# Eleven Strassen pairs instead of eight, their weight sums formed by adding transfers, in a two-layer decoder trunk

## The chip, the cores and the metric

One core of one Trainium2 chip runs the whole program; the other cores are idle. The metric is device microseconds of one execution. The kernel before takes 1021.03 us, the median of three runs (1020.96 to 1021.89).

## The reference, cut to what matters

Two layers over 256 tokens of width 1024, all in fp32. Each layer is a half-step SwiGLU feed-forward, a token mixer beside a cross-attention to a memory, and a second half-step SwiGLU; a last RMSNorm follows. The change touches the four feed-forwards and the first and last microseconds.

```python
D_MODEL, SEQ, DEPTH, D_FF = 1024, 256, 2, 2816

def rmsnorm(x, g, eps=1e-6):
    return x * lax.rsqrt(jnp.mean(x * x, axis=-1, keepdims=True) + eps) * g

def swiglu(h, w_up, w_down):
    gate, up = jnp.split(h @ w_up, 2, axis=-1)
    return (jax.nn.silu(gate) * up) @ w_down

for i in range(DEPTH):
    x = x + 0.5 * swiglu(rmsnorm(x, norm_g[i, 0]), ffn_w_up[i, 0], ffn_w_down[i, 0])
    h = rmsnorm(x, norm_g[i, 1])
    x = x + mixer(h, mem)        # layer 0: causal pooling, layer 1: differential attention
    x = x + 0.5 * swiglu(rmsnorm(x, norm_g[i, 2]), ffn_w_up[i, 1], ffn_w_down[i, 1])
return rmsnorm(x, final_norm_g)
```

## The kernel before, in words

**Precision.** Every fp32 weight and activation is split into hi (rounded to fp32r by ScalarE) and lo (the rest, by VectorE). A product is three matmuls: hi by hi, hi by lo, lo by hi (`mm3`, L474).

**Weights.** They arrive in pieces of 1 MiB (128 partitions x 2048 floats), issued on SyncE's queue into three buffers named `raw`, and are split in two halves of 1024 columns each, a CAST on ScalarE and a subtraction on VectorE, into one of four pairs of buffers `hi` and `lo` (`WB = 4`). So a split may run ahead of its use by four pieces at most. The class `Weights` (L248) keeps the queue of pieces.

**A feed-forward** has eleven chunks of 256 hidden columns. A `single` chunk (L855) takes two pieces of up-projection and 48 matmuls of 512 columns, for both halves of the tokens. Its gate (Silu on ScalarE, a multiply on VectorE) is transposed and split, and a `down` step (L846) of one piece and 24 matmuls adds the chunk to the four accumulators.

**A pair** (L758) does two chunks by seven products instead of eight (a Strassen-Winograd scheme over 2 token halves, 2 halves of the inner dimension and 2 chunks): 7 x 12 = 84 matmuls where two singles take 96. With the four weight blocks b11, b12 (first inner half of the two chunks), b21 and b22 (second half), product 1 takes b11, 5 takes b11+b12, 6 takes b11+b12+b22, 4 takes the sum of all four, 7 takes b12+b22, 2 takes b21 and 3 takes b22. VectorE forms these sums in place, eight additions of 1024 columns for a pair (L442, L1356), in four blocks held in three borrowed activation buffers (`ROOM`, tags `qk` and `mq`) and one `raw`. The activations have five sums of their own (`column_sums`, L581), which need both halves' `rstd`, the row scale of RMSNorm, made from a sum of squares by two small instructions on GpSimd (L484). Each feed-forward has two pairs (`steps`, L886): eight in all.

**The order of the work.** PE, ScalarE, VectorE and SyncE run in the order in which Python emits instructions. A planner (`Clock`, L57, with a duration for each kind of instruction, and `Flow`, L197) decides that order from chains of steps with due times. GpSimd's order is left to a scheduler of its own. A tile's readers and writers wait for each other through semaphores.

**Begin and end.** `begin` (L917) runs eight warm-up matmuls on zeros while the first pieces land (`BEGIN`, `BEGIN_X`, L44). At the end `accumulate` (L667) makes the last 512 columns of each token half in two parts of 256, and `last` (L1325) adds, squares and scales each part.

Of the kernel before, what the change touches and what calls it, by code (L numbers as in the profile page):

```python
# [18 lines left out]
P = 128  # L19
# [19 lines left out]
HOLD_PIECE = "hold"  # L39
# [3 lines left out]
WARM = 8  # L43
BEGIN = ((0, 1), (1, 2), (2, 4), (4, 8))  # L44
BEGIN_X = {0: (1, 4), 2: (4, 8)}
MARGIN = 0.25
LEFT = 384
BACKLOG = 0.3
# [81 lines left out]
class Engine:  # L130
# [117 lines left out]
class Weights:  # L248
# [3 lines left out]

    def __init__(self, flow, load, run, free):
        self.flow, self.load, self.run, self.free = flow, load, run, free
        self.queue, self.raw, self.done = [], {}, {}
        self.loaded = self.started = self.live = 0
        self.running = False
        self.open = []

    def add(self, key, src, tag="raw", pre=None, post=None, frees=("raw",)):  # L260
        self.queue.append((key, src, tag, pre, post, frees))

    def give(self, **tags):
        self.free.update(tags)
        self.pump()

    def pump(self):
        while self.loaded < len(self.queue):
            key, src, tag = self.queue[self.loaded][:3]
            if src is not None:  # L270
                if not self.free[tag]:
                    break
                self.free[tag] -= 1
                self.raw[key] = self.load(key, src, tag)
            self.loaded += 1
        if self.running or self.started >= self.loaded:
            return
        key, _, _, pre, _, _ = self.queue[self.started]
        if pre is HOLD_PIECE:
            self.started += 1  # L280
            self.pump()
            return
        if isinstance(key, tuple):
# [4 lines left out]
        self.flow.add(self.first(self.queue[self.started]))  # L288

    def first(self, entry):  # L290

        key, _, _, pre, _, _ = entry
        if pre:
            yield from self.after(key)
        self.open.append(key)
        raw, before = pre(self.raw) if pre else (self.raw.get(key), None)
        rest = yield from self.run(key, raw, before)
        self.started += 1
        self.running = False
        self.flow.add(self.second(entry, rest))  # L300
        self.pump()

    def after(self, key):

        while self.open and self.open[0] != key:
            yield self.flow.now + 0.05

    def second(self, entry, rest):
        key, _, _, _, post, frees = entry
        self.done[key] = yield from rest  # L310
        if post:
            yield from self.after(key)
            yield from post(self.raw)
        self.open.remove(key)
        for tag in frees:
# [14 lines left out]
def trunk(ctx, tc, I, out):  # L330
# [69 lines left out]
    def raw_tile(tag="raw"):  # L400
        if tag == "raw":
            return wp.tile([P, PIECE], F32, tag="raw", name=nm("raw"), bufs=RB)
        return act.tile([P, PIECE], F32, tag=tag, name=nm("raw"), bufs=ROOM[tag])
# [14 lines left out]
    def load(key, src, tag):  # L418
        if key == "x":
            for t in range(NT):  # L420
                nc.sync.dma_start(x[:, t, :], src[:, t, :])
            return None
        raw = raw_tile(tag)
# [8 lines left out]
    def split_piece(key, raw, before):  # L432
# [23 lines left out]
    W = Weights(F, load, split_piece, {"raw": RB, "none": 1, **ROOM})  # L456
# [163 lines left out]
    def finish_part(t, s, i, ss, y, fg):  # L620

        xs = x[:, t, s]
        junk = tmp.tile([P, D], BF16, tag="junk", name=nm("junk"), bufs=1)
        nc.scalar.activation(junk[:, s], xs, AF.Square, scale=D ** -0.5, accum_out=ss[:, i:i + 1])
        nc.vector.tensor_mul(y[:, s], xs, fg[:, s])

    def finish(t, ss, y):
        v = sm.tile([P, 2], F32, tag="v2", name=nm("v"))
        r = sm.tile([P, 1], F32, tag="rstd", name=nm("rstd"))
        nc.gpsimd.tensor_scalar(v[:, 0:1], ss[:, 0:1], EPS, ss[:, 1:2], op0=ALU.add, op1=ALU.add)  # L630
        nc.gpsimd.tensor_scalar(v[:, 1:2], ss[:, 2:3], v[:, 0:1], None, op0=ALU.add)
# [35 lines left out]
    def accumulate(acc, t, lh, ll, pc, k0, first, end=None):  # L667


        fine = end is last  # L670
        for i in range(4):
            kk, h = (i % 2, i // 2) if end else (i // 2, i % 2)
            if fine and h == 1:
                break
# [3 lines left out]
            if end and kk == 1:  # L678
                end(t, acc[t], h) if not fine else end(t, acc[t], h, None)
        for part in range(2 if fine else 0):  # L680
            o = slice(part * FC, part * FC + FC)
            w = slice(512 + part * FC, 512 + part * FC + FC)
            for kk in range(2):
                mm3(acc[t][1][:, o], lh[:, k0 + kk, cols(t)], ll[:, k0 + kk, cols(t)], pc[0][:, kk, w], pc[1][:, kk, w],
                    False, kk == 1, part == 1)
                F.poll()
            end(t, acc[t], 1, part)

    def exp_table():
        nc.scalar.activation(dcol2, dcol, AF.Exp)  # L690
        yield F.now

    def ffn(layer, f, end, begin=None, exp_next=False):
# [64 lines left out]
        def pair(a, *between):  # L758
# [63 lines left out]
            downs(between[0])  # L822
# [3 lines left out]
            downs(between[1])  # L826
# [35 lines left out]

        if begin:
# [22 lines left out]
    def steps(begin):  # L886


        if begin:
            return [("single", 1), ("down", 0), ("single", 2), ("down", 1), ("single", 3), ("pair", 4, 2, 3), ("single", 6),  # L890
                    ("down", 4), ("pair", 7, 5, 6), ("single", 9), ("down", 7), ("single", 10), ("down", 8, 9, 10)]
        return [("single", 0), ("single", 1), ("down", 0), ("single", 2), ("pair", 3, 1, 2), ("single", 5),
                ("down", 3, 4), ("single", 6), ("pair", 7, 5, 6), ("single", 9), ("down", 7), ("single", 10),
                ("down", 8, 9, 10)]

    def out_proj(cat, name, chain_ids, end):
# [8 lines left out]
        W.give(**ROOM)  # L905
# [11 lines left out]
    def begin():  # L917
# [11 lines left out]
        nc.scalar.dma_start(xr2[:, 0:SEQ], I["x_cols"][:, 0:SEQ])  # L929
        nc.scalar.activation(silu, mhalf[:, 0:1], AF.Silu)  # L930
        for i, (k0, k1) in enumerate(BEGIN):
            s = slice(k0 % 4 * 512, (k1 - 1) % 4 * 512 + 512)
            nc.sync.dma_start(raw[k0 // 4][:, s], I["ffn_w_up"][0, 0, 0, k0 // 4][:, s])
            if i in BEGIN_X:
                s = slice(BEGIN_X[i][0] * SEQ, BEGIN_X[i][1] * SEQ)
                nc.sync.dma_start(xr2[:, s], I["x_cols"][:, s])
        for k in range(KT):
# [216 lines left out]
    def pool_mix(end):  # L1154
        W.free.update(qk=0, mq=0)
# [123 lines left out]
    def diff_mix(end):  # L1279
        W.free.update(qk=0, mq=0)  # L1280
# [44 lines left out]
    def last(t, acc, h, part):  # L1325

        if h == 0:
            outs[t] = (sm.tile([P, 3], F32, tag="ss3", name=nm("ss3"), bufs=2), raw_tile()[:, 0:D])
        s = half(0) if h == 0 else slice(512 + part * FC, 512 + part * FC + FC)
        a = acc[h] if h == 0 else acc[h][:, part * FC:part * FC + FC]  # L1330
        nc.vector.scalar_tensor_tensor(x[:, t, s], a, 0.5, x[:, t, s], op0=ALU.mult, op1=ALU.add)
        finish_part(t, s, h + (part or 0), *outs[t], gains[0])
        if part == 1:
            finish(t, *outs[t])

    def plan_ffn(layer, f, begin=False):
# [6 lines left out]
        def pair(a, *between):  # L1343


            key = (layer, f, "pair", a)
            b11, b12, b22, b21 = [key + (n,) for n in (1, "b12", "b22", 2)]

            def plus(of, other):
                return lambda raw: (raw[of], raw[other])  # L1350

            def all_four(raw):
                for s in range(0, PIECE, SPLIT):
                    sl = slice(s, s + SPLIT)
                    yield max(at(raw[b21][:, sl], raw[b11][:, sl]), idle("dve"))
                    nc.vector.tensor_add(raw[b21][:, sl], raw[b21][:, sl], raw[b11][:, sl])  # L1356

            W.add(b11, up[layer, f, a, 0], "qk", frees=())
            W.add(b12, up[layer, f, a + 1, 0], "qk", HOLD_PIECE)
            W.add(key + (5,), None, pre=plus(b11, b12), frees=())  # L1360
            W.add(b22, up[layer, f, a + 1, 1], "mq", HOLD_PIECE)
            downs(between[0])
            W.add(key + (6,), None, pre=plus(b11, b22), frees=())
            downs(between[1])
            W.add(b21, up[layer, f, a, 1], post=all_four, frees=("qk",))
            W.add(key + (7,), None, pre=plus(b12, b22), frees=("qk",))
            W.add(key + (3,), None, pre=lambda raw: (raw[b22], None), frees=("mq",))
            W.add(key + (4,), None, pre=lambda raw: (raw[b21], None))

        for kind, *js in steps(begin):  # L1370
# [7 lines left out]
            if begin and kind == "single" and js[0] == 1:  # L1378
                W.add("x", I["x"].rearrange("b (t p) d -> p (b t) d", p=P), "none", frees=())
# [98 lines left out]
```

## Time and profile before

| | |
|---|---|
| median of three runs | 1021.03 us |
| the profiled execution | 1020.7 us |
| its span on the core | 1019.0 us |
| granted TensorE clock, mean | 0.996 |
| DMA, mean over the span | 185 GB/s |

The profile is of one execution. A row of busy time gives the microseconds in which an engine executed something, its share of the span and its instructions. A matmul row on PE shows how long the instruction was in the pipeline (some 0.39 us for 512 columns); consecutive ones overlap, so what one costs is read from a run of them in the chain of waits. PEclk is the granted share of TensorE's clock. In a timeline, brackets hold the idle time before an instruction and what ended it.

### The profile page before, as it was taken

The page shows a single profiled execution, that of the slowest core. Times are in us where ns is not written, and L with a number is a line of the kernel's source. Part 1 is how long each engine was busy: PE and PEld are TensorE (multiplying, and loading weights), DVE is VectorE, ACT ScalarE, POOL GpSimd, SP SyncE. Part 2 cuts the span into 40 slices and gives each one's busy share as a digit, 9 for nine tenths or more (in the row PEclk, how much of TensorE's full clock was granted, in tenths as well). Part 3 has the DMA queues.
Part 4 walks back from the last instruction along what each step waited for, and adds up shares of the span by engine and source line. Part 5 has one row for each costly group of instructions (what it writes and reads, how often), then busy time and mean ns, then how long its engine had stood idle before and what let it go on. Part 6 is the DMA issues. An engine that isn't in the chain of part 4 may idle for free.

```text
span 1019.0 us, 13188 instructions
## 1 busy us (share of the span) xinstructions
PE 1004.6 (99%) x5084; PEld 850.0 (83%) x5084; DVE 766.3 (75%) x1011; ACT 599.3 (59%) x949; POOL 66.1 (6%) x125
## 2 busy tenths in 40 slices
PE   8999999999999999999999999999999999999996
PEld 7888888899888888888888888889998888888885
DVE  5989896675768886975889698555776768987963
ACT  6656565864666564656646465563676575665642
POOL 1000072200000000000000000010211000000000
PEclk9999999999999999999999999999999999999999
DMA  9745445655437255374824627444424445273341
GB/s 355 279 164 230 172 165 209 233 184 191 168 138 289 83 218 214 111 261 146 330 83 161 252 100 272 165 169 175 152 98 156 170 169 237 83 307 146 131 179 42
DMA packets 27407, 188.19 MB, mean 185 GB/s; under 512 B 3152, under 2 KB 3664, under 8 KB 5200
## 3 DMA queue, kind: packets, MB, share of 16 engines
q1 hardware_dynamic: 26768, 186.79, 49.3%
q8 instruction: 40, 0.66, 0.3%
q10 hardware_dynamic: 576, 0.56, 0.2%
q14 instruction: 23, 0.19, 0.1%
HBM read 186.29 MB, written 1.05 MB: 184 GB/s over the span
## 4 chain that ended last, share of the span: by engine, by line
PE 94%; DVE 2%; ACT 1%; POOL 1%; issue 1%; DMA 1%; POOLq 0%; ACTq 0%
PE mm L146 51%; PE acc L146 32%; PE tr L146 11%; DVE lo L146 1%; ACT ds L146 1%; DMA x_cols<-in_x_cols 1%; DVE ds L146 0%; ACT junk L146 0%; POOL rs L146 0%; DVE x_res L146 0%; POOL nmx L146 0%; DVE dw L146 0%; DVE on L146 0%; DVE cat_lo L146 0%; DVE raw L146 0%
## 5 line engine op out<-in xcount | busy, mean ns | idle before, releaser
L146 DVE TENSOR_TENSOR lo<-raw,hi 128x1024 fp32r<-128x1024 f32 (+1 forms) x398 | 470.9, 1211 | 104.8 <-ACT hi L146 104.0
L146 ACT CAST hi<-raw 128x1024 fp32r<-128x1024 f32 (+1 forms) x398 | 400.1, 1039 | 206.5 <-DVE raw L146 73.2
L146 PE MATMUL mm<-hi,xT 128*128 128x512 f32 x1120 | 357.5, 392 | 0.0
L146 PEld LDWEIGHTS mm<-hi,xT 128*128 128x128 f32 x1120 | 210.3, 188 | 43.0
L146 PE MATMUL mm<-lo,xT 128*128 128x512 f32 x560 | 218.0, 389 | 0.0
L146 PE MATMUL acc<-hi,gh 128*128 128x512 f32 (+1 forms) x356 | 140.1, 393 | 2.3 <-DVE x_res L146 2.3
L146 PE MATMUL acc<-hi,gl 128*128 128x512 f32 (+1 forms) x356 | 138.0, 388 | 0.0
L146 PE MATMUL acc<-lo,gh 128*128 128x512 f32 (+1 forms) x356 | 137.8, 387 | 0.0
L146 PEld LDWEIGHTS mm<-lo,xT 128*128 128x128 f32 x560 | 105.2, 188 | 21.0
L146 PEld LDWEIGHTS acc<-hi,gh 128*128 128x128 f32 x356 | 66.9, 188 | 15.5 <-DVE x_res L146 2.7
L146 PEld LDWEIGHTS acc<-hi,gl 128*128 128x128 f32 x356 | 66.8, 188 | 13.8
L146 PEld LDWEIGHTS acc<-lo,gh 128*128 128x128 f32 x356 | 67.0, 188 | 13.0
L146 DVE TENSOR_TENSOR raw<-raw,raw 128x1024 f32<-128x1024 f32 x64 | 76.4, 1226 | 0.0
L146 PE MATMUL mm<-xT,hi 128*128 128x256 f32 x384 | 72.0, 288 | 1.1 <-DVE mq L146 1.1
L146 PEld LDWEIGHTS mm<-xT,hi 128*128 128x128 f32 x384 | 59.6, 191 | 2.9 <-issue 1.3
L146 POOL TENSOR_SCALAR v<-ss 128x1 f32<-128x1 f32 (+1 forms) x24 | 8.9, 370 | 740.9 <-ACT junk L146 740.7
L146 ACT ACTIVATE g<-mm,rstd 128x256 f32<-128x256 f32 x62 | 29.3, 473 | 44.2 <-PE mm L146 44.1
L146 PE MATMUL mm<-xT,lo 128*128 128x256 f32 x192 | 54.3, 283 | 0.0
L146 ACT CAST gh<-tr 128x256 fp32r<-128x256 f32 (+1 forms) x60 | 26.8, 480 | 46.6 <-PE tr L146 46.6
L146 DVE SCALAR_TENSOR_TENSOR g<-mm,rstd,g 128x256 f32<-128x256 f32 x62 | 29.8, 480 | 31.6 <-ACT g L146 31.6
L146 DVE TENSOR_TENSOR gl<-tr,gh 128x256 fp32r<-128x256 f32 (+1 forms) x60 | 31.2, 542 | 14.8 <-ACT gh L146 14.7
L146 PE MATMUL acc<-hi,cat_hi 128*128 128x512 f32 x96 | 38.4, 400 | 0.0
(183 smaller groups left out, 1234.4 us busy)
## 6 DMA issues: line engine op xcount, KB each, us to landing
raw<-in_ffn_w_up SPq DMA_DIRECT2D x87, 1024.0 KB, 4.9
raw<-in_ffn_w_down SPq DMA_DIRECT2D x44, 1024.0 KB, 4.9
raw<-in_diff_w_in SPq DMA_DIRECT2D x14, 1024.0 KB, 4.8
raw<-in_mem_w_kv SPq DMA_DIRECT2D x8, 1024.0 KB, 4.8
raw<-in_pool_w_in SPq DMA_DIRECT2D x6, 1024.0 KB, 4.8
raw<-in_pool_w_out SPq DMA_DIRECT2D x6, 1024.0 KB, 4.8
raw<-in_diff_w_out SPq DMA_DIRECT2D x6, 1024.0 KB, 4.8
x_res<-in_x SPq DMA_DIRECT2D x2, 512.0 KB, 7.8
```

Of the source, the lines that this page charges most:

```text
L146: return call(*args, **kwargs)
```

## The change

It does five things. (1) `steps` has three pairs instead of two in each feed-forward but the first, so eleven in all; two down steps stand between products of every pair, as before. (2) The sums of weights are made by transfers: SyncE loads one block, and a transfer issued by GpSimd adds another block to it in SBUF (`accum_op=ALU.add`). Block sum 5 grows into 6 and then into 4, each addition being issued when the sum before it has been split; sum 7 has a buffer of its own. The blocks b11, b21 and b22 are loaded by themselves as well. VectorE's additions are gone. (3) `begin` loads the first columns of x ahead of the first weights, in finer pieces, all on SyncE, and nine warm-up matmuls run. (4) The last 512 columns are done whole. (5) The planner has a duration for the adding transfer.

```diff
+WARM = 9
+BEGIN = (("x", 0, 1), ("w", 0, 1), ("w", 1, 2), ("x", 1, 2), ("w", 2, 4), ("x", 2, 4), ("w", 4, 6), ("x", 4, 8),
+         ("w", 6, 8))
+SUMS_FROM = 35.0
...
+        if op == "dma_start" and "accum_op" in kwargs:
+            t = c.run("pool", 1.2, outs, ins) + 9.0
+            c.mark(t, t, outs, ins)
+            return
...
-            if before is not None:
-                yield max(at(raw[:, sl], before[:, sl]), idle("dve"))
-                nc.vector.tensor_add(raw[:, sl], raw[:, sl], before[:, sl])
...
+    def weight_sums(layer, f, a, before):
+        up = I["ffn_w_up"][layer, f]
+        key = (layer, f, "pair", a)
+        def begun(tag, n, first, second):
+            t = act.tile([P, PIECE], F32, tag=tag, name=nm("sum_w"), bufs=ROOM[tag])
+            nc.sync.dma_start(t, up[first])
+            nc.gpsimd.dma_start(t, up[second], accum_op=ALU.add)
+            W.raw[key + (n,)] = t
+            return t
+        def ended(*keys):
+            while not all(k in W.ended for k in keys):
+                yield F.now + 0.2
+        if len(before) > 1:
+            yield from ended(before[-2] + (4,))
+        x1 = begun("qk", 5, (a, 0), (a + 1, 0))
+        if before:
+            yield from ended(before[-1] + (7,))
+        begun("mq", 7, (a + 1, 0), (a + 1, 1))
+        for n, then, other in ((5, 6, (a + 1, 1)), (6, 4, (a, 1))):
+            yield from ended(key + (n,))
+            nc.gpsimd.dma_start(x1, up[other], accum_op=ALU.add)
+            W.raw[key + (then,)] = x1
...
+        pairs = [step[1] for step in steps(begin) if step[0] == "pair"]
+        for i, a in enumerate(pairs):
+            F.add(weight_sums(layer, f, a, [(layer, f, "pair", p) for p in pairs[:i]]), SUMS_FROM if begin else 0)
...
-        return [("single", 0), ("single", 1), ("down", 0), ("single", 2), ("pair", 3, 1, 2), ("single", 5),
-                ("down", 3, 4), ("single", 6), ("pair", 7, 5, 6), ("single", 9), ("down", 7), ("single", 10),
-                ("down", 8, 9, 10)]
+        return [("single", 0), ("single", 1), ("pair", 2, 0, 1), ("single", 4), ("down", 2), ("pair", 5, 3, 4),
+                ("single", 7), ("down", 5), ("pair", 8, 6, 7), ("single", 10), ("down", 8, 9, 10)]
...
+    def last(t, acc, h):
         if h == 0:
+            outs[t] = (sm.tile([P, 2], F32, tag="ss2", name=nm("ss2")), raw_tile()[:, 0:D])
+        add_half(t, acc, h, 0.5)
+        finish_half(t, h, *outs[t], gains[0])
+        if h == 1:
             finish(t, *outs[t])
```

On GpSimd, at the start of the second feed-forward (`ss` is a half's sum of squares, `rstd` its row scale), there stood before:

```order
L146 TENSOR_SCALAR v_2627<-ss_2625 128x1
L146 TENSOR_TENSOR rstd_2628<-v_2627,mhalf 128x1
L146 TENSOR_SCALAR v_2702<-ss_2700 128x1
L146 TENSOR_TENSOR rstd_2703<-v_2702,mhalf 128x1
L146 TENSOR_SCALAR v_4014<-ss_4012 128x1
```

and now (`sum_w` is a block sum in the making; 2650 and 2656 become the sums 5, 6 and 4 of the first and the second pair, 2653 becomes sum 7 of the first):

```order
L147 TENSOR_SCALAR v_2626<-ss_2624 128x1
L147 TENSOR_TENSOR rstd_2627<-v_2626,mhalf 128x1
L147 DMA sum_w_2650<-in_ffn_w_up 128x2048
L147 DMA sum_w_2653<-in_ffn_w_up 128x2048
L147 DMA sum_w_2656<-in_ffn_w_up 128x2048
L147 TENSOR_SCALAR v_2710<-ss_2708 128x1
L147 TENSOR_TENSOR rstd_2711<-v_2710,mhalf 128x1
L147 DMA sum_w_2650<-in_ffn_w_up 128x2048 x2
```

Three adding transfers have come between the row scales of the two token halves.

On ScalarE, in the first pair of the second feed-forward, the casts of the sums 5 and 6 (both named `raw_2715`, summed in place) stood before among these:

```order
L146 CAST hi_2905<-raw_2715 128x1024 x2
L146 ACTIVATE g_2937<-mm_2907,rstd_2628 128x256
L146 CAST hi_2954<-raw_2752 128x1024 x2
L146 ACTIVATE g_2976<-mm_2938,rstd_2703 128x256
L146 CAST hi_2974<-raw_2715 128x1024
L146 ACTIVATE m_455_2977<-mm_2979,rstd_2628 128x512
L146 CAST hi_2974<-raw_2715 128x1024
```

and now, in the second pair, the casts of its sums 5, 6 and 4 (all `sum_w_2656`) with what is queued behind each:

```order
L147 CAST hi_3175<-sum_w_2656 128x1024 x2
L147 CAST hi_3194<-raw_3080 128x1024
L147 ACTIVATE g_3197<-mm_3151,rstd_2711 128x256
L147 CAST hi_3194<-raw_3080 128x1024
L147 CAST gh_3211<-tr_3222 128x512
L147 ACTIVATE m_500_3240<-mm_3242,rstd_2627 128x512
L147 CAST hi_3238<-sum_w_2656 128x1024
L147 COPY m_501_3241<-mm_3255 128x512
L147 CAST hi_3238<-sum_w_2656 128x1024
L147 CAST hi_3276<-raw_3117 128x1024 x2
L147 CAST hi_3295<-raw_3145 128x1024 x2
L147 CAST hi_3312<-sum_w_2984 128x1024 x2
```

A cast that waited for VectorE's addition now waits for a transfer to land, and ordinary casts stand behind it.

On SyncE, the first loads stood before in this order (512 columns of `raw` are one of eight slices of the first chunk's weights; the first 256 columns of `x_cols` came on ScalarE's queue):

```order
L146 DMA raw_111<-in_ffn_w_up 128x512
L146 DMA x_cols<-in_x_cols 128x768
L146 DMA raw_111<-in_ffn_w_up 128x512
L146 DMA raw_111<-in_ffn_w_up 128x1024
L146 DMA x_cols<-in_x_cols 128x1024
L146 DMA raw_112<-in_ffn_w_up 128x2048
```

and now:

```order
L147 DMA x_cols<-in_x_cols 128x256
L147 DMA raw_112<-in_ffn_w_up 128x512 x2
L147 DMA x_cols<-in_x_cols 128x256
L147 DMA raw_112<-in_ffn_w_up 128x1024
L147 DMA x_cols<-in_x_cols 128x512
L147 DMA raw_113<-in_ffn_w_up 128x1024
L147 DMA x_cols<-in_x_cols 128x1024
L147 DMA raw_113<-in_ffn_w_up 128x1024
```

The first slice of x has moved to the head of SyncE's queue, and the long loads behind it are cut.

## Rows read from the trace of the kernel before

**Rows 1.** The page's busy times: engine, us, share, instructions.

```profile
PE 1004.6 (99%) x5084; PEld 850.0 (83%) x5084; DVE 766.3 (75%) x1011; ACT 599.3 (59%) x949; POOL 66.1 (6%) x125
...
L146 DVE TENSOR_TENSOR raw<-raw,raw 128x1024 f32<-128x1024 f32 x64 | 76.4, 1226 | 0.0
```

**Rows 2.** Who PE waited for: total us, times, longest.

```profile
PE acc L146 <- ACT xT L146: 2.3, 1, 2.3
PE acc L146 <- DVE x_res L146: 2.3, 2, 1.1
PE tr L146 <- DVE warm L146: 1.1, 1, 1.1
PE mm L146 <- DVE mq L146: 1.1, 1, 1.1
PE tr L146 <- DVE on L146: 1.0, 2, 0.6
```

**Rows 3.** Chain of waits in the second feed-forward: start us, us, instructions.

```profile
345.55 5.44 PE acc L146 x24
```

**Rows 4.** The second feed-forward: PE, PEld, DVE, ACT, POOL busy, clock, DMA share, GB/s.

```profile
299.35:480.99 181.64, 181.64 (x836) 150.56 (x833) 144.79 (x162) 107.54 (x150) 2.18 (x5) 1.00 0.51 191
```

**Rows 5.** Transfers: queue with packets, MB, busy share; issues with us to landing.

```profile
q1 hardware_dynamic: 26768, 186.79, 49.3%
...
raw<-in_ffn_w_up SPq DMA_DIRECT2D x87, 1024.0 KB, 4.9
```

**Rows 6.** Stretches of the start, columns as in rows 4.

```profile
4.70:7.00 2.30, 0.00 (x1) 0.00 (x0) 0.67 (x2) 0.51 (x1) 0.00 (x0) 1.00 0.98 298
7.00:11.30 4.30, 4.30 (x12) 3.27 (x13) 3.50 (x7) 2.99 (x6) 0.00 (x0) 0.60 1.03 422
```

**Rows 7.** Timeline of the start: start us, us, engine, instruction, idle before.

```profile
1.23 0.45 ACTq L146 DMA_DIRECT2D x_cols<-in_x_cols  x1
...
4.01 0.62 ACT L146 CAST hi<-raw 128x512 fp32r<-128x512 f32 x1 [0.80 <-DMA raw<-in_ffn_w_up]
...
6.44 0.51 ACT L146 ACTIVATE xT<-x_cols,gcol 128x256 fp32r<-128x256 f32 x1 [1.82 <-DMA x_cols<-in_x_cols]
...
7.00 0.50 PE L146 MATMUL acc<-hi,xT 128*128 128x512 f32 x1 [2.30 <-ACT xT L146]
...
16.39 3.88 ACT L146 CAST hi<-raw 128x1024 fp32r<-128x1024 f32 x4
```

**Rows 8.** Timeline of the end.

```profile
1004.54 0.39 PE L146 MATMUL acc<-hi,gh 128*128 128x256 f32 x1 [1.14 <-DVE x_res L146]
...
1009.47 0.28 PE L146 MATMUL acc<-hi,gh 128*128 128x256 f32 x1
...
1009.66 0.69 DVE L146 SCALAR_TENSOR_TENSOR x_res<-acc,x_res 128x512 f32<-128x512 f32 x1 [1.37 <-PE acc L146]
...
1010.39 0.63 ACT L146 ACTIVATE junk<-x_res 128x512 bf16<-128x512 f32 x1 [2.04 <-DVE x_res L146]
...
1013.68 0.29 POOL L146 TENSOR_SCALAR v<-ss,v 128x1 f32<-128x1 f32 x1 [1.26 <-ACT junk L146]
```

**Rows 9.** GpSimd and PE at the second feed-forward's start.

```profile
299.78 0.57 POOL L146 TENSOR_TENSOR rstd<-v,mhalf 128x1 f32<-128x1 f32 x1
306.14 0.19 POOL L146 TENSOR_SCALAR v<-ss 128x1 f32<-128x1 f32 x1 [5.79 <-ACT junk L146]
...
308.09 0.60 PE L146 MATMUL tr<-ident,rstd 128*128 128x128 f32 x4
...
342.17 0.39 PE L146 MATMUL mm<-hi,sum_hi 128*128 128x512 f32 x1
```

**Rows 10.** VectorE there: first activation sum, then additions and split of weight sum 5.

```profile
317.78 0.68 DVE L146 TENSOR_TENSOR sum_lo<-sum,sum_hi 128x512 fp32r<-128x512 f32 x1
...
329.18 2.35 DVE L146 TENSOR_TENSOR raw<-raw,raw 128x1024 f32<-128x1024 f32 x2
331.59 2.36 DVE L146 TENSOR_TENSOR lo<-raw,hi 128x1024 fp32r<-128x1024 f32 x2
```

More of the change, by code (lines that the diff above doesn't have):

```diff
@@ L38 @@
 RB = 3
-HOLD_PIECE = "hold"
 T2K = 8
@@ L254, in __init__, with add @@
         self.flow, self.load, self.run, self.free = flow, load, run, free
-        self.queue, self.raw, self.done = [], {}, {}
+        self.queue, self.raw, self.done, self.ended = [], {}, {}, set()
         self.loaded = self.started = self.live = 0
         self.running = False
[L258 to L265, printed above, removed]
+    def add(self, key, src, tag="raw"):
+        self.queue.append((key, src, tag))
     def pump(self):
         while self.loaded < len(self.queue):
-            key, src, tag = self.queue[self.loaded][:3]
+            key, src, tag = self.queue[self.loaded]
             if src is not None:
@@ L273, in pump @@
                 self.free[tag] -= 1
-                self.raw[key] = self.load(key, src, tag)
+                self.raw[key] = self.load(key, src)
             self.loaded += 1
@@ L277, in pump @@
             return
[L278 to L283, printed above, removed]
+        if isinstance(self.queue[self.started][0], tuple):
             if self.live == WB:
@@ L287, in pump, with first, second @@
         self.running = True
[L288 to L297, printed above, removed]
+        self.flow.add(self.first(*self.queue[self.started]))
+    def first(self, key, src, tag):
+        while key not in self.raw:
+            yield self.flow.now + 0.1
+        rest = yield from self.run(key, self.raw[key])
         self.started += 1
         self.running = False
-        self.flow.add(self.second(entry, rest))
+        self.flow.add(self.second(key, src, tag, rest))
         self.pump()
[L303 to L309, printed above, removed]
-        self.done[key] = yield from rest
[L311 to L315, printed above, removed]
+    def second(self, key, src, tag, rest):
+        self.done[key] = yield from rest
+        self.ended.add(key)
+        if src is not None and tag == "raw":
             self.free[tag] += 1
@@ L415, in half, with load @@
         return slice(h * 512, (h + 1) * 512)
-    def load(key, src, tag):
+    def load(key, src):
         if key == "x":
@@ L430, in idle, with split_piece @@
         return clock.free[engine] - BACKLOG
-    def split_piece(key, raw, before):
+    def split_piece(key, raw):
         if not isinstance(key, tuple):
@@ L454, in split_rest @@
         return hi, lo
-    W = Weights(F, load, split_piece, {"raw": RB, "none": 1, **ROOM})
+    W = Weights(F, load, split_piece, {"raw": RB, "x": 1})
     special = {}
@@ L618, in column_sums, with finish_half @@
         split_lo(lo[:, 4], hi[:, 4], quarter[1][1], -1.0)
-    def finish_part(t, s, i, ss, y, fg):
-        xs = x[:, t, s]
+    def finish_half(t, h, ss, y, fg):
+        xs = x[:, t, half(h)]
         junk = tmp.tile([P, D], BF16, tag="junk", name=nm("junk"), bufs=1)
-        nc.scalar.activation(junk[:, s], xs, AF.Square, scale=D ** -0.5, accum_out=ss[:, i:i + 1])
-        nc.vector.tensor_mul(y[:, s], xs, fg[:, s])
+        nc.scalar.activation(junk[:, half(h)], xs, AF.Square, scale=D ** -0.5, accum_out=ss[:, h:h + 1])
+        nc.vector.tensor_mul(y[:, half(h)], xs, fg[:, half(h)])
     def finish(t, ss, y):
@@ L678, in accumulate @@
             if end and kk == 1:
[L679 to L687, printed above, removed]
+                end(t, acc[t], h)
     def exp_table():
@@ L821, in pair @@
             third = take_now()
-            downs(between[0])
+            downs(*between[:1])
             product(6, third, *summed(1), True)
@@ L825, in pair @@
             u2 = F.add(less("u2", third, kept["m1"]))
-            downs(between[1])
+            downs(*between[1:])
             product(2, first, *plain(1), False)
@@ L928, in begin @@
         nc.scalar.dma_start(gcol, I["gains"])
-        nc.scalar.dma_start(xr2[:, 0:SEQ], I["x_cols"][:, 0:SEQ])
         nc.scalar.activation(silu, mhalf[:, 0:1], AF.Silu)
[L931 to L935, printed above, removed]
+        for of, k0, k1 in BEGIN:
+            if of == "x":
+                s = slice(k0 * SEQ, k1 * SEQ)
                 nc.sync.dma_start(xr2[:, s], I["x_cols"][:, s])
+            else:
+                s = slice(k0 % 4 * 512, (k1 - 1) % 4 * 512 + 512)
+                nc.sync.dma_start(raw[k0 // 4][:, s], I["ffn_w_up"][0, 0, 0, k0 // 4][:, s])
         for k in range(KT):
@@ L1346, in pair @@
             key = (layer, f, "pair", a)
[L1347 to L1368, printed above, removed]
+            W.add(key + (1,), up[layer, f, a, 0])
+            W.add(key + (5,), None)
+            downs(*between[:1])
+            W.add(key + (6,), None)
+            downs(*between[1:])
+            W.add(key + (2,), up[layer, f, a, 1])
+            W.add(key + (7,), None)
+            W.add(key + (3,), up[layer, f, a + 1, 1])
+            W.add(key + (4,), None)
         for kind, *js in steps(begin):
@@ L1378, in plan_ffn @@
             if begin and kind == "single" and js[0] == 1:
-                W.add("x", I["x"].rearrange("b (t p) d -> p (b t) d", p=P), "none", frees=())
+                W.add("x", I["x"].rearrange("b (t p) d -> p (b t) d", p=P), "x")
     def plan_in(name, c):
```

30 lines of the change are left out of this document (6 added, 24 removed).

## The prediction

> **What bounds the kernel now.** I read the busy times first. PE is busy for 1004.6 of 1019.0 us, VectorE for 75% of the span [rows 1]. A matmul is in the pipeline longer than it costs, so next comes who PE waited for: five causes, 7.8 us in all, the longest 2.3 us [rows 2]. The chain of waits then gives what a matmul costs: 24 of 512 columns take 5.44 us, 0.227 us each [rows 3]. In the second feed-forward PE has no idle time at all in 181.64 us, at full clock, while the transfers take 51% of their engines [rows 4]. So the middle of the kernel is bound by the number of matmuls. Only the first 20 and the last 15 us have waits worth removing. VectorE's 76.4 us of weight additions [rows 1] are beside PE's work: no wait of PE names them [rows 2].
>
> The sum is made against the profiled execution: 1020.7 us, of which 1019.0 are the span. That is 0.3 us under the median of the runs.
>
> **Matmuls.** A pair has 84 matmuls of 512 columns where two singles have 96. Three pairs more remove 36: 36 x 0.227 = -8.2 us. Transposes stay as many. PE has no idle time in that stretch, so all of it counts, if operands keep coming.
>
> **The start.** PE's first useful matmul stood at 7.00, after 2.30 us of idle time: the first slice of x, issued on ScalarE's queue at 1.23, held up its split until 6.44, while the weights had been there since 4.01 [rows 7]. Now x goes first and the weights second on SyncE's queue. If a slice takes from issue to landing what the weights' slice took (issued about 0.8, cast at 4.01), both are there at about 4.5. The cast, 0.62, and x's split, 0.51, bring PE's start to about 5.6: -1.4 us. Behind the idle time the granted clock was 0.60 for 4.30 us, in which 12 matmuls started that need 2.7 us at full clock: 1.6 us lost [rows 6]. The ninth warm-up matmul pair ends some 0.4 us before the new start, and I expect the clock to stay at 2.4 GHz: -1.6. That is -3.0 together, and the other end is nothing: the next chunk's pieces were cast from 16.39 on [rows 7] behind transfers at 422 GB/s [rows 6], and if they come no sooner, PE waits for them instead. I take -2.5, nearer the first end, since the new cuts let ScalarE begin each slice sooner.
>
> **The end.** The two parts of 256 columns share an accumulator, and in each token half PE waited 1.14 us until VectorE had read the first part (the two x_res waits) [rows 2, 8]. Done whole, this goes: -1.1 in the first half. In the second, six matmuls of 512 columns from 1009.47 end at about 1011.0 instead of the last part's end behind the wait. VectorE's addition, 0.69, gives 1011.8, the square, 0.63 with its read-out inside 0.8, gives 1012.6, and GpSimd's row that stood at 1013.68 [rows 8] starts near 1012.7: -1.0. Twelve matmuls for 24 half ones save 0.1. Together -2.2 us.
>
> **Earlier sums of activations.** Product 5 of the first pair comes 72 matmuls, 16.3 us, sooner after the feed-forward's start: at 342.17 - 16.3 = 325.8 in the times of before. It needs the first sum only, ready at 318.5 [rows 9, 10], 7.3 us to spare. ScalarE and VectorE are fuller there, so I put +1 us on it (0 to 2).
>
> **Adding transfers.** The trace has none. What they carry: a three-pair feed-forward has 36 MiB of plain loads (10 for singles, 11 for downs, 15 for pairs) and 12 MiB of additions, where before it had 33 MiB. Those took 0.51 x 181.64 = 92.6 us of the engines [rows 4], 2.81 us each, and over the whole run 2.82 [rows 5]. If an addition costs as a plain load, 48 x 2.81 = 135 us of 178.9, 75%. If it costs two, 60 x 2.81 = 169 us, 94%.
>
> What they hold up: PE reaches product 6 one product and one down step after product 5, 36 matmuls or 8.2 us, and the split of sum 5 can run ahead by four buffers: before, it ended at 333.95 for a product at 342.17, 8.2 us [rows 9, 10]. From that end to product 6 there are 16.4 us, of which the first half's cast and subtraction need some 2.3. An addition so has about 14 us from issue to landing before PE waits. From sum 6 to product 4 lie 72 matmuls, 16.3 us, and the budget is about 16. ScalarE waits sooner: its cast of the sum stands in order, with casts of ordinary pieces and gates behind it.
>
> The landing lies between 4.9 us, a plain MiB [rows 5], and 4.9 + 2.8 (a second read) + 5.6 (two plain loads sharing the engines) = 13.3, to which GpSimd's issue comes, not in the trace, of the order of its other rows, 0.2 to 2 us: 15 at most. I take 11, nearer the upper end, since at 75 to 94% load an addition seldom runs alone. That is inside the budgets on average. I put +3 us for the places where several queue up, above all the first feed-forward, whose three first sums start together while eight loads are in flight. Below nothing is excluded: no PE wait is left that an addition could take away.
>
> What the trace shows is the load of plain transfers alone, 51% [rows 4]. The Trainium skill ("Collectives: The Full Stack", The bandwidth ceiling: the fold count and why AG ≠ RS ≠ AR) says that a reduction in the transfer engines runs at half a copy's rate, not because of the add but because it needs two source reads. By it the load is the 94% of above, with the landing near my 11 to 13 us. By one read it is 75%, and the +3 falls to 0. No run here shows which yet.
>
> **Sum.** 1020.7 - 8.2 - 2.5 - 2.2 + 1 + 3 = 1011.8. I predict 1012 us. The likeliest case's own range is 1008 to 1017.
>
> **Rivals.**
>
> A, the other side: the additions become the bound. Place: product 6 and product 4 of each pair. Price: at a landing of 17 us, product 6 waits 3 us and product 4 one, 4 us a pair, 44 us over eleven: 1008.8 + 44 = 1053. It decides for slower from a landing of about 15 us, where one wait of 1.1 us a pair makes 12 us and eats the gain. Longer waits cost more than themselves: after PE's 2.30 us of idle time the clock stood at 0.60 [rows 6], while after 1.14 us nothing shows. For it: the 94%, only three plain buffers, and ScalarE's order. Against it: the load stays under 100% even so, at 422 GB/s [rows 6] a MiB takes only 2.5 us, and a plain piece has most of the four buffers' lead in hand. The skill's rule on two reads leads here if a read from SBUF is no quicker than one from HBM. A landing of 16.4 us, 2.4 us a pair, gives 1035, the middle of it.
>
> B: an addition costs as much as a plain load. Then it lands in 5 to 8 us, no budget is touched, and the time is 1008.8, near 1009. For it: the block it adds to is on the chip already. Against it: the destination must be read as well as written.
>
> C: GpSimd's queue. Between the row scales of the two token halves stand three additions now, each waiting for its plain load. The second scale's first instruction ran at 306.14, 5.8 us after the first scale was done. With a power of 0.57 like the first's it was ready near 307.0, and PE took both at 308.09, 1.1 us later [rows 9]. The loads are issued early enough, but if an addition held GpSimd for 3 us, the three would end 3.2 us late, 2.1 behind PE's need, in three feed-forwards: +6 us, 1018.
>
> D: the change does less than it says at the start, because PE waits for the second chunk's pieces. That is inside the range: +2.5.
>
> **Chances.** Forecast 0.45, A 0.22, B 0.25, C 0.08. A measurement of this kernel tells 0.2%, about 2 us, from no change, so faster is under 1019.0 and slower over 1023.1. Faster: 0.41 of the forecast, of which 0.04 is left for a miss upwards, all of B and half of C, 0.70. Within the bound: those 0.04 and 0.03 of A's lower edge, 0.07. Slower: the rest of A and of C, 0.23. The range for 8 in 10 runs from 1006, B with the full gain of the start, to 1035, the middle of A.
>
> **What would show it.** PE must show 36 matmuls fewer in 512-column equivalents. The first useful matmul must stand near 5.6 with the clock at 1.00 behind it. The wait for x_res must be gone, and GpSimd's last rows must come a microsecond earlier after the last 512 columns begin. The three-pair feed-forwards must take about 179 us. Who PE waits for must not show a subtraction of `lo` from `sum_w` in microseconds per pair. If it does, the issue table's time to landing of `sum_w` says by how far the additions passed 14 and 16 us, and the DMA share of the feed-forwards tells one read (0.75) from two (0.94). I am wrong if PE's waits in the middle exceed 12 us in sum.

## The result, and the profile after

The changed kernel takes 1068.01 us (median of four runs, 1067.08 to 1069.19), the kernel before 1021.45 us beside it: ratio 1.0457 (95% interval 1.0441 to 1.0473). It is 47 us slower, where 9 us faster were forecast, and 33 us above the upper end of the range.

The page of the changed kernel shows busy times, transfer queues and issues (columns as in [rows 1, 5]); q0 is GpSimd's queue, the adding transfers, and q1 SyncE's, the plain ones:

```profile
PE 1015.9 (95%) x5038; PEld 851.3 (80%) x5038; DVE 722.4 (68%) x982; ACT 619.1 (58%) x975; POOL 101.3 (10%) x169
...
q1 hardware_dynamic: 28784, 198.46, 48.3%
q0 software_dynamic: 6336, 46.14, 22.2%
...
raw<-in_ffn_w_up SPq DMA_DIRECT2D x75, 1024.0 KB, 8.3
raw<-in_ffn_w_down SPq DMA_DIRECT2D x44, 1024.0 KB, 8.4
sum_w<-in_ffn_w_up POOLq DMA_DIRECT2D x44, 1024.0 KB, 11.2
```

The work is less, as planned: PE has 46 instructions fewer (36 fewer for the pairs and 12 at the end, two more for the warm-up). An addition landed after 11.2 us in the median, the 11 of the prediction. But each took 0.222 x 1065.6 / 44 = 5.38 us of the 16 engines, a plain MiB 0.483 x 1065.6 / 189.3 = 2.72: a ratio of 1.98, the price of two loads and not of one. The rule of the Trainium skill ("Collectives: The Full Stack", The bandwidth ceiling: the fold count and why AG ≠ RS ≠ AR), half a copy's rate for a reduction, agrees with this ratio. And the plain pieces, which landed after 4.9 us before [rows 5], now took 8.3.

The first, second, third and fourth feed-forward (columns as in [rows 4]):

```profile
0.00:202.10 202.10, 192.81 (x850) 157.24 (x851) 139.69 (x176) 118.86 (x170) 34.49 (x59) 0.97 0.80 264
311.00:505.60 194.60, 184.23 (x821) 151.24 (x821) 136.11 (x159) 114.39 (x160) 12.77 (x17) 0.97 0.82 259
505.60:702.50 196.90, 184.82 (x822) 151.14 (x821) 136.07 (x159) 114.24 (x161) 12.66 (x17) 0.97 0.79 246
869.00:1058.40 189.40, 180.78 (x809) 148.03 (x807) 131.57 (x157) 106.66 (x149) 13.16 (x19) 0.98 0.76 234
```

All four are longer (before they took 190.7, 181.6, 181.6 and 183.3 us), the second by 13 us against [rows 4], though it has 12 matmuls fewer. PE's busy time is shorter than the stretch, and the clock, 1.00 in [rows 4], is 0.97. PE's waits (us in total, times, longest; compare [rows 2]), then ScalarE's waits for transfers:

```profile
PE tr L147 <- DVE m L147: 21.4, 5, 5.0
PE tr L147 <- ACT hi L147: 4.9, 4, 2.2
PE tr L147 <- DVE u L147: 4.8, 5, 1.9
PE tr L147 <- DVE g L147: 3.1, 1, 3.1
PE tr L147 <- DVE lo L147: 3.0, 4, 0.8
```

```profile
ACT hi L147 <- DMA raw<-in_ffn_w_up: 48.2, 15, 7.7
ACT hi L147 <- DMA sum_w<-in_ffn_w_up: 46.0, 16, 6.8
...
ACT hi L147 <- DMA raw<-in_ffn_w_down: 13.4, 9, 3.2
```

The largest wait of PE names `m`, a gate that VectorE finishes. That is the last link. The timeline at one of the five (start us, us, instruction, idle before) shows what stands ahead of it:

```profile
377.40 1.99 ACT L147 CAST hi<-raw 128x1024 fp32r<-128x1024 f32 x2 [7.12 <-DMA raw<-in_ffn_w_up]
...
379.30 0.41 ACT L147 ACTIVATE m<-m 128x256 f32<-128x256 f32 x1
...
379.75 0.43 DVE L147 TENSOR_TENSOR m<-m 128x256 f32<-128x256 f32 x1
...
380.23 0.69 PE L147 MATMUL tr<-ident,m 128*128 128x128 f32 x2 [4.47 <-DVE m L147]
```

ScalarE stood 7.12 us at the cast of an ordinary piece that had not landed. Behind that cast, in ScalarE's order, stood the gate's Silu, whose result had nothing to do with that piece. VectorE's multiply and PE's transposition followed at once. The piece had been issued at 364.79 and took 12.5 us to land. After the 4.9 us of before [rows 5] it would have been there at 369.7, before ScalarE was free for it at 370.28. Two adding transfers, issued at 365.74 and 370.72, were in flight beside it. At the other four waits ScalarE stood 5.80, 7.21, 5.88 and 7.65 us at such a cast with the same Silu behind it. The stretches around this one (columns as in [rows 4]):

```profile
367.50:375.75 8.25, 8.25 (x38) 6.38 (x36) 4.96 (x7) 2.62 (x4) 0.86 (x1) 1.00 1.03 318
375.75:380.23 4.48, 0.01 (x2) 0.01 (x1) 1.65 (x2) 2.83 (x6) 0.00 (x0) 0.96 1.03 294
380.23:383.30 3.07, 3.07 (x10) 2.59 (x11) 2.94 (x6) 1.04 (x4) 0.00 (x0) 0.50 1.02 264
```

The transfer engines are full (a share of 1.02 to 1.03) at only 264 to 318 GB/s, since an addition takes them twice as long for the bytes that are counted. PE idles 4.48 us, and then the granted clock is 0.50 (1.2 GHz) for 3.07 us.

### The profile page after: what moved, and what is told of

Its sections match the earlier page's. It is cut to its first block, busy times and chain, and to the rows that moved or that the text cites. A ratio compares the mean times of both kernels' runs of the same rounds, so it can differ in the third digit from the quotient of the medians.

```text
span 1065.6 us, 13245 instructions
## 1 busy us (share of the span) xinstructions
PE 1015.9 (95%) x5038; PEld 851.3 (80%) x5038; DVE 722.4 (68%) x982; ACT 619.1 (58%) x975; POOL 101.3 (10%) x169
## 3 DMA queue, kind: packets, MB, share of 16 engines
q0 software_dynamic: 6336, 46.14, 22.2%
## 4 chain that ended last, share of the span: by engine, by line
PE 65%; DMA 18%; DVE 9%; ACT 4%; issue 2%; POOL 1%; SPq 0%; POOLq 0%; ACTq 0%
PE mm L147 31%; PE acc L147 25%; DMA sum_w<-in_ffn_w_up 10%; PE tr L147 9%; DMA raw<-in_ffn_w_up 8%; DVE lo L147 6%; ACT hi L147 3%; DVE xg L147 1%; DVE g L147 1%; ACT ds L147 1%; DVE ds L147 0%; DVE u L147 0%; ACT junk L147 0%; DVE x_cols L147 0%; DVE m L147 0%
## 5 line engine op out<-in xcount | busy, mean ns | idle before, releaser
L147 DVE TENSOR_TENSOR lo<-raw,hi 128x1024 fp32r<-128x1024 f32 (+1 forms) x328 | 390.2, 1210 | 95.3 <-ACT hi L147 94.9
L147 ACT CAST hi<-raw 128x1024 fp32r<-128x1024 f32 (+1 forms) x328 | 327.0, 1037 | 143.8 <-PE mm L147 51.3
L147 DVE TENSOR_TENSOR lo<-sum_w,hi 128x1024 fp32r<-128x1024 f32 x88 | 105.5, 1221 | 112.2 <-ACT hi L147 112.2
L147 ACT CAST hi<-sum_w 128x1024 fp32r<-128x1024 f32 x88 | 89.2, 1049 | 86.9 <-DMA sum_w<-in_ffn_w_up 46.0
L147 PE MATMUL acc<-hi,gh 128*128 128x512 f32 x352 | 139.1, 395 | 0.0
L147 PE MATMUL acc<-hi,gl 128*128 128x512 f32 x352 | 137.4, 390 | 0.0
L147 PE MATMUL acc<-lo,gh 128*128 128x512 f32 x352 | 137.3, 390 | 0.0
L147 PE MATMUL tr<-hi,sum_hi 128*128 128x512 f32 x132 | 53.3, 404 | 8.8 <-ACT hi L147 4.9
L147 PE MATMUL tr<-lo,sum_hi 128*128 128x512 f32 x132 | 53.5, 405 | 3.0 <-DVE lo L147 3.0
L147 PE MATMUL tr<-hi,sum_lo 128*128 128x512 f32 x132 | 53.1, 402 | 0.0
## 6 DMA issues: line engine op xcount, KB each, us to landing
sum_w<-in_ffn_w_up POOLq DMA_DIRECT2D x44, 1024.0 KB, 11.2
```

Of the source, the lines that this page charges most:

```text
L147: return call(*args, **kwargs)
```

## The experiments

Theory 1: an adding transfer takes the transfer engines for two loads; they fill up, all pieces land late, and ScalarE, which casts in order, holds up what stands behind. Theory 2: it is GpSimd's queue, or the additional transfers as such. Theory 3: it is the new order, with three pairs and earlier sums of activations.

**The adds taken out, made plain, and halved.** In each of three kernels the planner still sees the whole addition, so PE, VectorE and ScalarE execute the changed kernel's order; only what the transfer carries differs (sums left out in part or whole). In short, with the additions that make the sums 6 and 4 changed alike:

```diff
-            nc.gpsimd.dma_start(t, up[second], accum_op=ALU.add)
+            nc.gpsimd.dma_start(t[:, 0:64], up[second][:, 0:64], accum_op=ALU.add)      # tiny_adds
+            nc.gpsimd.dma_start(t, up[second])                                          # plain_loads
+            nc.gpsimd.dma_start(t[:, 0:1024], up[second][:, 0:1024], accum_op=ALU.add)  # half_adds
```

> The changed kernel with each of the 44 adding transfers cut to 64 of its 2048 columns (so most of the sums of weights are left out); the order of PE, VectorE and ScalarE is word for word that of the changed kernel. Theory 1 (an adding transfer takes the transfer engines for two loads; they fill up, all loads land late, ScalarE's casts hold up what stands behind them): without the adds the load falls to about 57% of a feed-forward, plain loads land in 5 to 6 us again, PE waits under 12 us in sum, the clock is back at 0.99, time 1008 to 1014. Theory 2 (GpSimd's queue, its issue of 0.9 us and its place behind others is what costs): the 44 issues are still there, so 1040 or more. Theory 3 (the order with three pairs and earlier sums of activations is at fault): 1050 or more.

> The changed kernel with each adding transfer made a plain load of the same block by the same queue (the sums are left out); order as in the changed kernel. Theory 1: 48 MiB a feed-forward at one load each, 75% of the engines; landings of 6 to 9 us, a few PE waits, 1010 to 1025. Theory 2 (the queue of GpSimd or the 22 additional MiB of plain loads): as the changed kernel, 1055 to 1070.

> The changed kernel with each adding transfer cut to half its columns (half of the sums left out). Theory 1: half an add takes what one plain load takes (2.69 us of 16 engines), so the load is 75% as with plain loads, and the time is the same as there within 5 us, 1010 to 1028. Theory 2: as the changed kernel, 1055 or more. If adds cost by number and not by size, also 1055 or more.

| | us, median | ratio to before (95%) |
|---|---|---|
| adds of 64 columns | 1010.97 | 0.9900 (0.9884 to 0.9917) |
| plain loads | 1013.18 | 0.9919 (0.9905 to 0.9934) |
| adds of 1024 columns | 1011.15 | 0.9902 (0.9888 to 0.9917) |

All three came out as theory 1 has them. The queue, the issues, the additional plain blocks and this order together cost nothing that shows: with 64 columns the same order runs 57 us faster than the changed kernel. From the pages of the 64-column, the plain and the half kernel, in this order:

```profile
raw<-in_ffn_w_up SPq DMA_DIRECT2D x75, 1024.0 KB, 4.8
```

```profile
q0 software_dynamic: 6336, 46.14, 12.2%
...
raw<-in_ffn_w_up SPq DMA_DIRECT2D x75, 1024.0 KB, 6.4
```

```profile
q0 software_dynamic: 6336, 23.07, 12.8%
...
raw<-in_ffn_w_up SPq DMA_DIRECT2D x75, 1024.0 KB, 4.9
```

Forty-four halves of a MiB, added, hold the engines about as long as 44 whole MiB, loaded (12.8% and 12.2% of the span). At that load, 0.76 and 0.75 of the engines in the second feed-forward, both kernels are within 2.2 us of the one with hardly any added bytes. The second and the third feed-forward with 64 columns:

```profile
299.70:478.70 179.00, 179.00 (x822) 148.26 (x821) 135.98 (x160) 114.84 (x160) 12.87 (x17) 1.00 0.61 214
478.70:657.60 178.90, 178.90 (x822) 148.18 (x821) 135.90 (x159) 114.73 (x161) 12.61 (x17) 1.00 0.58 203
```

Against [rows 4] that is -2.6 and -2.7 us, twelve matmuls at 0.227, with no idle time of PE. Against the changed kernel it is -15.6 and -18.0.

**Transfers by themselves.** A kernel that computes nothing of the model, with plain and adding transfers of 1 MiB alone and side by side.

```python
def load(engine, t):
    engine.dma_start(t, block())
def add(t):
    nc.gpsimd.dma_start(t, block(), accum_op=ALU.add)
```

> No part of the model: transfers of 1 MiB by themselves, in phases (16 plain loads of SyncE; one of SyncE; one of GpSimd; one adding; 8 plain of GpSimd; 8 adding; 4 adding beside 8 plain of SyncE). Theory 1: one add lands some 2.7 us later than a plain load of the same queue; 8 adds take about 43 us (5.4 each), 8 plain ones of GpSimd about 21 us, and 4 adds beside 8 plain loads about 4 x 5.4 + 8 x 2.7 = 43 us. Theory 2: plain loads of GpSimd take as long as adds.

The phases overlapped, because the engines ran ahead of each other, so the times expected for whole phases can't be compared. I read stretches in which one kind, or a steady mix, is in flight. Plain loads of SyncE alone, 3 to 13 us:

```profile
q1 hardware_dynamic: 580, 4.23, 100.6%
```

Adds and plain loads side by side, 68.5 to 90.7 us:

```profile
q0 software_dynamic: 431, 3.14, 67.8%
q1 hardware_dynamic: 432, 3.15, 35.1%
```

One add at a time, 142.7 to 159.2 us:

```profile
q0 software_dynamic: 288, 2.10, 68.5%
...
t<-in_ffn_w_up POOLq DMA_DIRECT2D x2, 1024.0 KB, 8.0
```

Alone, plain loads move 423 GB/s, 2.48 us a MiB. Side by side the two queues get the same number of packets, but the adds hold the engines for two thirds of the time. So 22.2 us carry three MiB of each kind, 7.4 us for one of both, and the plain queue is down to 142 GB/s, a third. An add by itself lands in 8.0 us; the rest of the 11.2, and of the long ones, I put down to sharing. Theory 2 falls here too: plain loads of GpSimd share with SyncE's at 4.97 us for one of both, by the landings in the trace, twice 2.48.

**The other parts, alone and together, with VectorE's additions.**

```diff
# before_11pairs: steps() alone
-        return [("single", 0), ("single", 1), ("down", 0), ("single", 2), ("pair", 3, 1, 2), ("single", 5),
...
+        return [("single", 0), ("single", 1), ("pair", 2, 0, 1), ("single", 4), ("down", 2), ("pair", 5, 3, 4),
...
# before_start: first loads and warm-up alone
+WARM = 9
+BEGIN = (("x", 0, 1), ("w", 0, 1), ("w", 1, 2), ("x", 1, 2), ("w", 2, 4), ("x", 2, 4), ("w", 4, 6), ("x", 4, 8),
+         ("w", 6, 8))
# before_end: the last 512 columns whole, alone (before_all3 is the three together)
-        for part in range(2 if fine else 0):
...
+                end(t, acc[t], h)
```

> The kernel before with the changed list of steps alone: three pairs in three feed-forwards, VectorE's additions kept. Theory 1 (the adding transfers alone lost the time, the pairs are worth their matmuls): each of the three feed-forwards 2.6 us shorter, 1013 to 1014.5. Rival (the additions of one pair more, 9.8 us of VectorE a feed-forward, which is 80% busy there, hold up PE, so that the adding transfers were needed): 1018 or more, with PE waiting for lo.

> The kernel before with the changed first loads and nine warm-up matmuls alone. As predicted: -2.5, 1018.5 to 1019. Theory now (the start is ahead by 1 us at the 50th matmul, and the first feed-forward ends no sooner, because ScalarE and VectorE then hold PE up elsewhere): 1020.5 to 1021.5.

> The kernel before with the last 512 columns done whole, alone. As predicted: -2.2, 1019 to 1019.6. Rival (the longer tail of 512 columns eats it): within 0.5 of before.

> The kernel before with the changed steps, first loads and end, but VectorE's additions in place of the adding transfers. Theory 1: the sum of the other three, 1010 to 1012, as fast as the changed kernel with its adds cut to 64 columns (1011.0). Rival (VectorE too full): 1016 or more.

| | us, median | before beside it | ratio (95%) |
|---|---|---|---|
| eleven pairs | 1022.13 | 1020.92 | 1.0011 (1.0002 to 1.0019) |
| start | 1020.03 | | 0.9991 (0.9982 to 1.0000) |
| end | 1018.54 | | 0.9979 (0.9970 to 0.9988) |
| all three | 1017.50 | | 0.9963 (0.9951 to 0.9976) |

The end is worth what was forecast. The start is worth 0.9, with an interval that reaches to nothing, and lies between the two expectations. The pairs are a miss of my theory: with VectorE's additions kept, three in a feed-forward give nothing, and the three changes together stand at the rival's 1016 or more. The second feed-forward of the eleven-pair kernel, what its weight loads waited for, and VectorE around 342 us:

```profile
300.60:482.20 181.60, 180.49 (x822) 147.94 (x821) 162.87 (x184) 113.41 (x160) 2.22 (x5) 1.00 0.50 189
```

```profile
PEld tr L146 <- DVE lo L146: 6.4, 9, 1.0
PEld mm L146 <- DVE lo L146: 3.3, 6, 0.6
```

```profile
340.89 4.62 DVE L146 TENSOR_TENSOR raw<-raw,raw 128x1024 f32<-128x1024 f32 x4
345.63 1.22 DVE L146 TENSOR_TENSOR lo<-raw,hi 128x1024 fp32r<-128x1024 f32 x1
```

VectorE is busy for 162.87 of 181.60 us, 90%, where it had 144.79 [rows 4]. Its additions in a row delay the `lo` of the pieces behind them. The waits are short (1.0 us at most) and stand mostly before weight loads, 9.7 us over three feed-forwards. So PE still looks busy while each takes 181.6 us and not 179.0, 2.6 us more. The rival was right: VectorE's additions, free with two pairs, are not free with three.

**The first pair later.** Steps in which three singles and a down step precede the first pair, otherwise `before_all3`.

```diff
-        return [("single", 0), ("single", 1), ("pair", 2, 0, 1), ("single", 4), ("down", 2), ("pair", 5, 3, 4),
-                ("single", 7), ("down", 5), ("pair", 8, 6, 7), ("single", 10), ("down", 8, 9, 10)]
+        return [("single", 0), ("single", 1), ("down", 0), ("single", 2), ("pair", 3, 1, 2), ("single", 5),
+                ("pair", 6, 3, 4), ("down", 5), ("pair", 8, 6, 7), ("single", 10), ("down", 8, 9, 10)]
```

> As the version with VectorE's additions and all three other parts (1017.5), but the first pair stands behind three singles and a down step, where it stood before; the two others follow closer. Theory (VectorE is full only where the first pair's additions meet the activations' sums): 1010 to 1013. Rival (VectorE at about 85% of such a feed-forward is late wherever three pairs stand): 1016 to 1019.

1023.02 us, ratio 1.0016 (1.0007 to 1.0025): worse than the rival's 1016 to 1019. So the first pair's place alone was not the cause: VectorE was busy for 89% of the second feed-forward here too, and late at this place as well. That it came out worse because the other two pairs stand closer is likely and not shown.

**One pair of three by transfers.** The first pair of the three later feed-forwards takes its sums from adding transfers, 12 in all; the rest stays with VectorE.

```diff
+        if not begin:
+            F.add(weight_sums(2))
...
+            if a == 2:
+                W.add(key + (1,), up[layer, f, a, 0])
+                W.add(key + (5,), None, "sum", frees=())
...
+                return
```

> Eleven pairs, changed first loads and end; the sums of weights of the first pair of the three later feed-forwards by adding transfers, all others by VectorE. Theory 1 (VectorE is full where the first pair stands, the transfer engines are full where every pair adds by transfer; a third of each leaves room in both): load 65%, PE waits as with the adds cut, 1010 to 1012.5. Rival (an adding transfer holds up the chain from sum 5 to 6 to 4 by its own length, whatever the load): 1016 or more.

1010.26 us (1009.94 to 1010.75), ratio 0.9891 (0.9878 to 0.9905): faster than the kernel before and the changed one. Its second feed-forward, and its queues and landings:

```profile
299.20:478.20 179.00, 179.00 (x822) 148.36 (x821) 154.56 (x175) 114.55 (x160) 6.01 (x9) 1.00 0.63 223
```

```profile
q0 software_dynamic: 1728, 12.58, 6.5%
...
sum_w<-in_ffn_w_up POOLq DMA_DIRECT2D x12, 1024.0 KB, 9.6
```

The transfers are at 63%, VectorE at 86%, and PE has no idle time. Twelve additions with a median landing of 9.6 us cost nothing here, which rules out the rival that an add costs by its own length.

**Fewer adds, and a longer planned landing.** The changed kernel with the steps of before (32 adds), and with a planned landing of 18 us instead of 9.

```diff
-            t = c.run("pool", 1.2, outs, ins) + 9.0
+            t = c.run("pool", 1.2, outs, ins) + 18.0
```

> The changed kernel with the steps of before: two pairs in each feed-forward, 32 adding transfers, which is 51 loads' worth or 76% of a feed-forward's engines. Theory 1: the first feed-forward loses its 11 us as in the changed kernel, the three others less than half of their 18 us; 1025 to 1045. Rival (each add costs the same whatever the load, 57 us over 44): 1018 + 32 x 1.3 = 1060.

> The changed kernel with the planner's time for an adding transfer 18 us in place of 9, which moves casts and pieces behind it. Theory 1 (the transfer engines are full for stretches): the order does not make bandwidth, 1050 to 1075. Rival (ScalarE's order alone is at fault, because the planner's landing is too short): 1020 to 1035.

With 32 adds 1040.76 us, ratio 1.0209 (1.0171 to 1.0246), inside what theory 1 gave. Its first three feed-forwards take 201.8, 184.8 and 184.5 us: the first is as long as in the changed kernel, the second and the third exceed before's 181.6 by 3 us instead of 13 and 15. The mean load does not decide it: the engines are at 0.76 in the second feed-forward here, as with the half adds, which cost nothing. Beside the order, the slowest plain piece of the feed-forwards differs, 23.0 us to landing here and 16.5 with the half adds (23.2 in the changed kernel). That a whole add holds its neighbours up for longer at a time fits this and is not shown by itself, since this order had no run with small adds.

With the longer plan the time is 1100.22 us, ratio 1.0769 (1.0752 to 1.0787): slower than both theories said. PE's waits and the landings:

```profile
PE tr L147 <- ACT hi L147: 25.2, 12, 6.8
PE tr L147 <- DVE u L147: 16.2, 11, 1.5
```

```profile
raw<-in_ffn_w_up SPq DMA_DIRECT2D x75, 1024.0 KB, 7.6
...
sum_w<-in_ffn_w_up POOLq DMA_DIRECT2D x44, 1024.0 KB, 10.3
```

The transfers landed sooner than in the changed kernel, and PE waited longer. The same two waits, 1.47 and 1.68 us, stand in each of the eleven pairs. So an order can be a cost of its own (the 64-column run clears only the changed kernel's), and waiting longer in the plan is no remedy. Which casts the plan holds back too long, I did not follow; whether another order would carry 44 adds is open.

## Why the prediction was wrong

**The step that failed** is "That is inside the budgets on average. I put +3 us for the places where several queue up". The term of 3 us measured 57: 1068.0 against 1011.0 for the same order with adds of 64 columns. The landing was right in the median, 11.2 us for the 11 I took, and so was the dearer of the two prices of an add. But a stall is made by the late ones. In the trace, 15 of the 44 adds landed after more than the 14 us of the budget, the slowest after 23.4. At the start of every feed-forward three were in flight together. The adds issued from 311 to 330 us (the median is the last number):

```profile
sum_w<-in_ffn_w_up POOLq DMA_DIRECT2D x4, 1024.0 KB, 17.1
```

My upper end of 15 counted one add and two plain loads. With three adds in flight and loads between them, the third of each start took 22.3 to 23.4.

**What it left out** is the other party. I priced the adds' landing alone and let the plain pieces keep theirs ("a plain piece has most of the four buffers' lead in hand"). The transfers by themselves show what an add does to its neighbours: at one packet each, the plain queue is left a third of its rate. ScalarE waited more for plain pieces (48.2 + 13.4 us) than for sums (46.0); with adds of 64 columns it was 11.0 and nothing.

**The account closes.** The changed kernel is 56.6 us over the same order with adds of 64 columns (spans 1065.6 and 1009.0). PE's waits, all rows, are 42.3 us against 5.0: 37 us. The mean clock is 0.981 against 0.999: 1065.6 x 0.019 - 1009.0 x 0.001 = 19 us. Together 56. PE's busy time agrees with the share of the clock: 1015.9 against 996.5, 19 us.

**Rival A** had the kind of it: a load near full, ScalarE's order, a clock that falls after long waits. Its place was too narrow (products 6 and 4, and not every piece behind them), and its price with it: 4 us a pair at a landing of 17 us and nothing at the 11.2 that was measured, where 57 us over eleven pairs are 5.2. Its sum for 16.4 us has a slip too: 2.4 us at product 6 and 0.4 at product 4 are 2.8 a pair, so 1040 and not 1035, still 28 us short. I held against it that the load stays under 100%. The mean load of a feed-forward did (0.76 to 0.82); in the five waits behind `m` it was 0.99 to 1.03. The sign that I had set, a share of 0.94 for two reads, did not show, because the feed-forward itself became longer: 0.82 of 194.6 us would be 0.89 of 179. B fell with the ratio of 1.98. C fell: an add holds GpSimd for 0.89 us on average, not 3.

**The other terms.** Matmuls: forecast -8.2, with the adds cut -2.6, -2.7 and, in the fourth feed-forward, -5.7 with the end: right. Its condition, "if operands keep coming", was the whole matter: with VectorE's additions they didn't (1022.13), so "VectorE's 76.4 us of weight additions are beside PE's work" held for two pairs and not for three. With the same steps, start and end, leaving VectorE's additions out is worth 1017.5 - 1011.0 = 6.5 us, of which the prediction had nothing. Earlier sums of activations: +1, measured 0 (the 179.0 us with 64 columns leave no room for it). End: -2.2, measured -2.4; in the changed kernel GpSimd's row stands 3.24 us after the last six matmuls begin (1060.03 after 1056.79), 4.21 before [rows 8]. Start: -2.5, measured -0.9. PE's first matmul was right (5.80 for 5.6), and so was the clock:

```profile
5.80 0.51 PE L147 MATMUL acc<-hi,xT 128*128 128x512 f32 x1 [0.87 <-ACT xT L147]
...
5.80:12.90 7.10, 6.71 (x25) 4.46 (x26) 4.95 (x10) 4.63 (x10) 0.00 (x0) 1.00 1.00 370
```

But the slices behind it came no sooner: with the new start alone the third slice of the weights landed at 9.23, before at 8.67. That is rival D in kind, at the first chunk's third slice and not at the second chunk's pieces. In the kernel with the new start alone:

```profile
9.25 0.62 ACT L146 CAST hi<-raw 128x512 fp32r<-128x512 f32 x1 [1.97 <-DMA raw<-in_ffn_w_up]
...
10.44 0.50 PE L146 MATMUL acc<-hi,xT 128*128 128x512 f32 x1 [1.20 <-ACT xT L146]
```

Starting 1.1 us earlier and at full clock, PE caught up with the transfers and waited for the third slice; its 50th matmul stands at 19.12, at 19.93 before.

## What to carry to other kernels

Before moving work from an engine to the transfers, write the load of the transfer engines per stage, with every add counted twice, and ask what it does to the transfers that are already there: beside a full queue of adds, a queue of plain loads dropped to a third. A mean load below 1 is no clearance, since 0.76 cost nothing with half adds and 3 us a feed-forward with whole ones. Judge a landing against a budget by its slow third and not by its median, and name what stands in order behind the instruction that waits. When one resource is too full either way, split the work: the sums of three pairs by transfer and of eight by VectorE took the whole gain of the extra pairs, which neither took alone.

## What the hardware showed

- Two full queues shared the transfer engines packet by packet (431 and 432 packets in 22.2 us), not by time: the queue with the dearer packets, the adds, took two thirds (67.8% against 35.1%).
- After a wait of 4.47 us PE's clock was granted at 0.50 (1.2 GHz) for the next 3.07 us. After two waits of 1.49 and 0.76 us close together it was 0.52 over the 3.5 us from 349.0. After single waits of 1.06, 1.76 and 1.87 us it stayed at 1.00 (2.4 GHz).
- VectorE at 90% cost PE 2.6 us a feed-forward in waits of at most 1 us, most of them seen only in the rows of the weight loads (eleven pairs); at 86%, with the first pair's sums by transfer, it cost none.
